# Attention ahead of S5 and GLA, with S5's weight-only matrices made in paced steps and kept in DRAM

## The chip, the cores and the metric

The kernel runs on one core of one Trainium2 chip. The metric is the device time of one execution in microseconds (us), as the median of several runs. The engines are TensorE (PE: matmuls, and PEld its weight loads), VectorE (DVE), ScalarE (ACT), GpSimd (POOL), and SyncE (SP), which issues nearly all DMAs.

## The reference

Two layers run over 640 tokens, 512 of a sample and 128 of a prompt, of width 1024. Each layer normalises, projects once into all inputs, runs three branches, gates and merges them:

```python
h = rms_norm(x, p['norm_w']) * (1.0 + scale) + shift
(gq, gk, gv, gaf, gab, g_gate, mq, mkv, mkr, m_gate, su, s_gate, merge) = split_cols(h @ p['w_in'], IN_SPLITS)
o_a, st_gla = gla_mixer(gq, gk, gv, gaf, gab, ..., ctx_gla)      # chunked linear attention, 4 heads
o_b, st_mla = mla_mixer(mq, mkv, mkr, ..., rope, ctx_mla)        # softmax attention, 4 heads
o_c, st_s5 = s5_mixer(su, ..., ctx_s5)                           # complex diagonal scan, then a GLU
g_a, g_b, g_c = jnp.split(jax.nn.sigmoid(merge), 3, axis=-1)
mixed = (g_a * ((o_a * jax.nn.silu(g_gate)) @ p['w_bo_gla'])
         + g_b * ((o_b * jax.nn.silu(m_gate)) @ p['w_bo_mla'])
         + g_c * ((o_c * jax.nn.silu(s_gate)) @ p['w_bo_s5']))
y = x + gate * (mixed @ p['w_out'])
```

S5 turns its weights (a, dt, B, C) into powers of the discretised a and products of those with B and C. These depend on no token. The three branches depend on `h` alone, so their order is free.

## The kernel before

Activations lie with the channels on the partitions, as 8 tiles of 128 x 640. Every f32 product is made of three matmuls of split values: `split` writes `hi` with ACT and `lo = x - hi` with DVE. Weights come as 128 x 512 halves (`wraw`, one DMA from `wpk`), and `half` splits each into `whi` and `wlo`. A projection `projh_` is 8 k-steps of 6 matmuls of 128 x 320 and yields after each k-step.

The order of TensorE is the order in which the program is written. The other engines and the DMA queue are ordered by a scheduler of the framework, which uses priorities and its own timeline. Where a branch is a chain of small dependent steps, the program calls `fill(n)`, which takes n k-steps from the generators in `self.stand`, so that TensorE has projections to do meanwhile. The tables `FILL`, `FM` (attention) and `FG` (GLA head) hold the n of each place.

The order in a layer is: `h`; the S5 input projection `s5_su`; the S5 kernel (`s5_kernel`: per group of channels C-outers `s5qk`, made by three DVE operations each, times `s5rd`); `s5_in`, `s5_z` (B-outers `s5r`, transposed), powers (`s5_pow`), scan (`s5_scan`), output (`s5_y`, from the matrices `s5m`, which pass through DRAM as `kd`, and `s5qy`, which pass as `qd`) and GLU; attention (`mla_qkv`, `mla_heads`); GLA (`gla_in`, four times `gla_head`); then `merge(0)` and `out_proj`. Filler is what the later branches need: latents and gates (`mla_raw`), eight merge gates (`mer_early(0)`), `merge(2)` along attention, `merge(1)` along GLA. While layer 0 runs `out_proj`, `s5_open(1)` makes the S5 coefficients of layer 1 and steps its `s5_kernel` three tiles in.

A GLA head goes: cumulated gates, exponentials `eb`, `kd`, `kr`, `fill(FG[0])`, scores `att`, `fill(FG[1])`, transposes of `kr`, `fill(FG[2])`, state products and the chain of 16 updates of `st` on DVE (each needs the one before in its direction), `fill(FG[3])`, output matmuls, norm `gon`, `fill(FG[4])`, transposes of `gon` into `og`.

Of the kernel before, what the change touches and what calls it, by code (L numbers as in the profile page):

```python
# [10 lines left out]
F32 = mybir.dt.float32  # L11
# [8 lines left out]
L = 2  # L20
# [4 lines left out]
NB = 16  # L25
# [159 lines left out]
FILL = (17, 2, 1, 4, 2, 10, 10, 1, 7, 3)  # L185
FM = (1, 6, 1, 4, 2, 4, 3, 2, 1)
FG = (7, 2, 2, 5, 5)
# [14 lines left out]
class Prog:  # L202
# [113 lines left out]
    def consts(self):  # L316
# [20 lines left out]
        self.qd = [self.dr.tile([8, 2, 128, 512], F32, name=f"qd{l}") for l in range(L)]  # L337
        self.sud = [self.dr.tile([NT, 512], F32, name=f"sud{l}") for l in range(L)]
        self.gd = [self.dr.tile([8, 128, NT], F32, name=f"gd{l}") for l in range(L)]
        self.md = [self.dr.tile([8, 128, NT], F32, name=f"md{l}") for l in range(L)]  # L340
# [136 lines left out]
    def gate_(self, name, og=False):  # L477
# [3 lines left out]
        if og:  # L481
            g = self.ogp.tile([128, NT], F32, name="og", tag="og", bufs=12)
        else:
            g = self.th.tile([128, NT], F32, name="gt", tag="gt", bufs=2)
        self.V.scalar_tensor_tensor(self.v2(g), self.v2(th), 1.0, ps, op0=ALU.add, op1=ALU.mult)
        return g
# [11 lines left out]
    def mer_early(self, b):  # L498

        for j in range(8):  # L500
            self.mid = True
            th = yield from self.mer(b, j)
            self.S.dma_start(self.md[self.l][j], th)
            self.early.add((b, j))
            self.mid = False
# [10 lines left out]
    def finish_tile(self, g):  # L516
        while self.mid:
            yield next(g)

    def merge(self, b, og, mode):  # L520
        V = self.V
        if mode:
            parts = []
            for t in og:
                hi, lo = self.og(), self.og()
# [4 lines left out]
        if mode == 0:  # L530
            self.mix = self.mx()[:, :5120].rearrange("p (k t) -> p k t", k=8)
        for j in range(8):
            if (b, j) in self.early:
                th = self.th.tile([128, NT], F32, name="th", tag="th", bufs=2)
                self.S.dma_start(th, self.md[self.l][j])
            else:
                th = yield from self.mer(b, j)
                yield True
            ps = yield from self.proj_([self.half(f"bo{b}_{j // 2}", j % 2)], og)
            m = self.mix[:, j, :]  # L540
            if mode == 0:
# [43 lines left out]
    def cmul(self, V, p, o_r, o_i, ar, ai, br, bi, shape):  # L585
        pat = "p (a b) -> p a b"
        t1 = p.tile([128, shape[1] * shape[2]], F32, name="cm1", tag="cm1")
        t2 = p.tile([128, shape[1] * shape[2]], F32, name="cm2", tag="cm2")
        t1, t2 = (t.rearrange(pat, a=shape[1]) for t in (t1, t2))
# [3 lines left out]
        t3 = p.tile([128, shape[1] * shape[2]], F32, name="cm1", tag="cm1")  # L593
        t4 = p.tile([128, shape[1] * shape[2]], F32, name="cm2", tag="cm2")
        t3, t4 = (t.rearrange(pat, a=shape[1]) for t in (t3, t4))
# [20 lines left out]
    def exp_(self, V, p, out, x):  # L616

        t = p.tile([128, 3, 64], F32, name="ex", tag="ex")
        k, r, y = t[:, 0], t[:, 1], t[:, 2]
# [8 lines left out]
        e = p.tile([128, 64], I32, name="exi", tag="exi")  # L628
# [3 lines left out]
    def s5_prep(self, l, vec, p, pz, ptmp):  # L632

        V = self.V
        n0 = VEC["B1"][0]
        bs, cs = pz.tile([128, 1024], F32, name="s5b"), p.tile([128, 1024], F32, name="s5c")
        with self.tc.high_priority(5200):
            for i, t in enumerate((bs, cs)):
                self.S.dma_start(t, self.a["vec"][l][:, n0 + 1024 * i:n0 + 1024 * i + 1024])
        self.B1, self.B2, self.C1, self.C2 = (t[:, 512 * i:512 * i + 512].rearrange("p (g c) -> p g c", c=16)  # L640
                                              for t in (bs, cs) for i in range(2))
# [992 lines left out]
```

## Time and profile before

| | before |
|---|---|
| median of 3 runs | 1600.47 us (1599.04 to 1603.54) |
| profiled execution | 1601.22 us, span 1599.4 us |
| mean granted TensorE clock | 0.981 |
| PE, DVE, ACT, POOL busy | 95%, 66%, 40%, 3% of the span |
| matmuls | 11334 |

The time of the profiled execution holds 1.8 us around the span. A busy PE is not a PE at its peak: matmuls are pipelined, so two that overlap count once, and at half clock the same matmuls are busy for longer. The granted clock is a mean over a stretch of the two levels 2.4 GHz (1.00) and 1.2 GHz (0.50).

### The profile page before, as it was taken

How to read it: one execution, taken by the hardware profiler on the slowest of the kernel's cores; microseconds unless marked ns; L12 is line 12 of the kernel's file. 1: busy time of each engine (PE TensorE's matmuls, PEld its weight loads, DVE VectorE, ACT ScalarE, POOL GpSimd, SP SyncE). 2: the span in 40 equal slices, each digit the busy share in tenths (PEclk: the TensorE clock that was granted, in tenths of full speed). 3: DMA queues.
4: the chain of work that ended last, by engine and by line, in shares of the span. 5: the costliest groups of instructions: out<-in, count | busy, mean ns of one | idle time of the engine just before them, and what ended most of it. 6: DMA issues, size and time to landing. Idle time of an engine off the chain costs nothing. (4 is left out here: it accounts for less than half of the span.)

```text
span 1599.4 us, 28779 instructions
## 1 busy us (share of the span) xinstructions
PE 1516.4 (95%) x11334; PEld 1438.9 (90%) x11334; DVE 1056.4 (66%) x2435; ACT 631.8 (40%) x1171; POOL 47.7 (3%) x48
## 2 busy tenths in 40 slices
PE   4999999999998898999799999999999989989999
PEld 3789999999997888898697999999999979889998
DVE  8986992367566436879987579724766663477762
ACT  3335223555444353333223542244544442634331
POOL 0000000012000000000000000000210000000000
PEclk9999999999999899999899999999999999999999
DMA  9451435323311121227553432442332122212253
GB/s 339 169 152 42 154 114 157 117 86 115 113 55 58 46 75 54 65 85 255 206 193 92 124 112 90 138 151 76 106 120 93 55 66 66 68 60 60 93 166 107
DMA packets 108792, 179.73 MB, mean 112 GB/s; under 512 B 12656, under 2 KB 30768, under 8 KB 108656
## 3 DMA queue, kind: packets, MB, share of 16 engines
q1 hardware_dynamic: 108656, 177.89, 34.3%
q8 instruction: 89, 1.46, 0.4%
q14 instruction: 47, 0.39, 0.1%
HBM read 149.23 MB, written 28.61 MB: 111 GB/s over the span
## 5 line engine op out<-in xcount | busy, mean ns | idle before, releaser
L245 PE MATMUL pj<-h,whi 128*128 128x320 f32 x3456 | 664.1, 313 | 0.0
L245 PEld LDWEIGHTS pj<-h,whi 128*128 128x128 f32 x3456 | 541.2, 189 | 6.6 <-issue 5.1
L227 ACT ACTIVATE whi<-wraw 128x512 fp32r<-128x512 f32 x326 | 205.0, 631 | 508.4 <-PE pj L245 359.2
L245 PE MATMUL pj<-h,wlo 128*128 128x320 f32 x1728 | 397.3, 310 | 0.0
L236 DVE TENSOR_TENSOR wlo<-wraw,whi 128x512 fp32r<-128x512 f32 x326 | 223.9, 688 | 245.5 <-ACT whi L227 238.6
L245 PEld LDWEIGHTS pj<-h,wlo 128*128 128x128 f32 x1728 | 290.3, 188 | 0.0
L245 PE MATMUL pj<-og,whi 128*128 128x320 f32 x736 | 142.1, 313 | 0.3 <-DVE og L236 0.3
L245 PEld LDWEIGHTS pj<-og,whi 128*128 128x128 f32 x736 | 114.7, 188 | 4.7 <-ACT whi L227 1.6
L245 PE MATMUL pj<-whi,h 128*128 128x512 f32 x256 | 87.1, 401 | 6.3 <-ACT h L230 5.7
L245 PE MATMUL pj<-og,wlo 128*128 128x320 f32 x384 | 87.5, 309 | 0.0
L245 PEld LDWEIGHTS pj<-whi,h 128*128 128x128 f32 x256 | 48.7, 192 | 19.5 <-ACT h L230 6.3
L245 PEld LDWEIGHTS pj<-og,wlo 128*128 128x128 f32 x384 | 64.2, 188 | 0.0
L230 ACT ACTIVATE P<-bank,smx 128x384 f32<-128x384 f32 x64 | 36.4, 575 | 56.0 <-DVE smx L1215 56.0
L236 DVE TENSOR_TENSOR Ptl<-bank,Pth 128x512 fp32r<-128x512 f32 x48 | 32.1, 689 | 34.3 <-ACT Pth L227 33.7
L230 ACT ACTIVATE th<-pj 128x640 f32<-128x640 f32 x72 | 49.6, 689 | 5.5 <-PE pj L245 5.4
L245 PE MATMUL pj<-wlo,h 128*128 128x512 f32 x128 | 50.8, 397 | 0.0
L245 PE MATMUL pj<-s5g,whi 128*128 128x320 f32 x256 | 48.1, 310 | 0.0
L245 PE MATMUL bank<-s5qy,mx 128*80 128x128 f32 x256 | 46.1, 302 | 0.0
L227 ACT ACTIVATE Pth<-bank 128x512 fp32r<-128x512 f32 x48 | 27.5, 596 | 41.3 <-PE bank L1236 41.1
L1236 PE MATMUL bank<-c,P 128*128 128x128 f32 x192 | 32.2, 304 | 11.9 <-ACT P L230 5.3
L1211 DVE TENSOR_REDUCE smx<-bank 128x1 f32<-128x384 f32 (+1 forms) x72 | 36.2, 524 | 9.0 <-PE bank L245 8.1
L1400 DVE SCALAR_TENSOR_TENSOR st<-st,bl,bank 64x128 f32<-64x128 f32 x112 | 38.9, 347 | 3.6
(349 smaller groups left out, 2324.2 us busy)
## 6 DMA issues: line engine op xcount, KB each, us to landing
wraw<-wpk SPq DMA_DIRECT2D x358, 256.0 KB, 2.7
og<-wpk SPq DMA_DIRECT2D x48, 256.0 KB, 5.1
qd<-s5qk SPq DMA_DIRECT2D x32, 256.0 KB, 2.2
s5qy<-qd SPq DMA_DIRECT2D x32, 256.0 KB, 4.1
gd<-gt SPq DMA_DIRECT2D x16, 320.0 KB, 2.5
gt<-gd SPq DMA_DIRECT2D x16, 320.0 KB, 3.1
md<-th SPq DMA_DIRECT2D x16, 320.0 KB, 2.3
th<-md SPq DMA_DIRECT2D x16, 320.0 KB, 3.1
```

Of the source, the lines that this page charges most:

```text
L227: self.A.activation(out, in_, AF.Copy, scale=scale)
L230: self.A.activation(out, in_, f, **kw)
L236: (eng or self.V).tensor_tensor(lo, src, hi.bitcast(F32), op=ALU.subtract)
L245: self.T.matmul(out, lhsT, rhs, start=start, stop=stop, skip_group_check=True, **kw)
L1211: V.tensor_reduce(mx[:, i:i + 1], ps[:, 0:w], axis=AX.X, op=ALU.max)
L1236: self.T.transpose(pt[:, nq * i + 128 * qi:nq * i + 128 * qi + 128], pr[qi][:, 128 * k:128 * k + 128], self.ident)
L1400: V.scalar_tensor_tensor(out, st[r, c, :], bl[r, c:c + 1], pu[c][r], op0=ALU.mult, op1=ALU.add)
```

## The change

The branches run in the order attention, S5, GLA. The latents are projected right behind `s5_su`, and everything else that `h` feeds (12 gates, 24 merge gates, the last third of the modulation) becomes filler from there on, stored to DRAM (`gd`, `md`) and loaded again by `gate_in` and `merge`. `merge(1)` and `merge(2)` are the filler of the GLA heads. `s5_ahead` makes all S5 matrices that depend on weights alone in about 134 steps per layer, paced by `bg`: 60 at the start of layer 0, then one per k-step of `s5_su`, 0.75 per step of the latents, 0.5 per filler step. It stores them to DRAM (`qd`, `rd`, `r0d`, `ptd`), and `s5_kernel`, `s5_z` and `s5_scan` load them. The groups of `s5_kernel` stand between the steps of the scan, and nothing of layer 1's S5 is made at the end of layer 0.

```diff
-FILL = (17, 2, 1, 4, 2, 10, 10, 1, 7, 3)
+FILL = (8, 2, 1, 3, 2, 10, 10, 1, 7, 3)
+COEF = 60
+PACE = (1, 0.75, 0.5)
 FM = (1, 6, 1, 4, 2, 4, 3, 2, 1)
-FG = (7, 2, 2, 5, 5)
+FG = (5, 2, 2, 4, 4)
...
+    def s5_ahead(self, l, vec, x):
...
+        def outers(m, coef, dst):
+            for n in range(16):
...
+                for _ in self.outer(V, v4(o[n % 2]), v4(o[2]), c[0], c[1], m[0][:, 4 * b:4 * b + 4], m[1][:, 4 * b:4 * b + 4], sh):
+                    yield
+                self.S.dma_start(dst[b, d], o[n % 2])
...
         for b in range(8):
-            q = [self.s5_q(V, p, b, d, f"s5qk{d}", 4) for d in range(2)]
+            q = []
             for d in range(2):
-                self.S.dma_start(self.qd[l][b, d], q[d].rearrange("p a b c -> p (a b c)"))
+                q.append(p.tile([128, 4, 8, 16], F32, name=f"s5qk{d}", tag=f"s5qk{d}", bufs=2))
+                self.S.dma_start(q[d], self.qd[l][b, d].rearrange("p (a b c) -> p a b c", a=4, b=8))
+            yield
...
+    def gates_(self):
+
+        for i in (0, 1, 2, 3, 8, 9, 10, 11, 4, 5, 6, 7):
+            g = yield from self.gate_(("mg%d", "gg%d", "sg%d")[i // 4] % (i % 4))
+            self.S.dma_start(self.gd[self.l][i], g)
+            self.gdone.add(i)
             yield True
...
     def fill(self, n):
 
         for _ in range(n):
+            self.bg(PACE[2])
...
+    def bg(self, n):
+
+        self.owed += n
+        while self.owed >= 1:
+            self.owed -= 1
+            next(self.ahead, None)
...
+        for _ in self.mla_raw():
+            self.bg(PACE[1])
+        self.stand = [self.gates_(), self.alternate(self.mer_early(1), self.ada(l, self.vec, 2)), self.mer_early(2), self.mer_early(0)]
+        fill(FILL[6])
...
                 ogb = self.mla_heads(p)
-        self.stand = [g for g in self.stand if g is not early] + [self.finish_tile(early)]
-        fill(1000)
-        self.stand = [self.merge(1, ogb, 1)]
-        fill(1)
+        run(self.ahead)
+        with ExitStack() as eg:
+            with pool("s5a") as pa:
+                with pool("s5k") as pk:
+                    kern = self.s5_kernel(pk)
+                    with pool("s5i") as p, tc.high_priority(2000):
+                        self.s5_in(pa, p, fill)
+                        self.s5_z(p, fill)
+                    with pool("s5s") as p:
+                        self.s5_pow(p)
+                        for n, _ in enumerate(self.s5_scan(p)):
+                            fill(FILL[3])
+                            if n % 2:
+                                next(kern, None)
+                        run(kern)
...
         with pool("gla") as pa:
             with pool("glb") as p:
                 self.gla_in(pa, p)
+            fill(1000)
+            part = lambda: self.hp.tile([128, NT], F32R, name="h", tag="h", bufs=16)
+            self.stand = [self.merge(1, ogb, part, True), self.merge(2, ogc)]
             with pool("glc") as p:
                 oga = [self.gla_head(p, h) for h in range(4)]
         fill(1000)
-        out = self.merge(0, oga, 2)
+        out = self.merge(0, oga, self.og)
...
-        self.s5_open(l + 1)
-        kern = self.s5[-1]
         run(self.alternate(out, self.ada(l + 1, self.nvec, 0)))
-        for j, _ in enumerate(self.out_proj()):
-            if j >= 3:
-                next(kern, None)
+        run(self.out_proj())
```

The first place is the end of the last attention head of layer 0 on TensorE: the last products with the probabilities (`Pth`, `Ptl`), the transpose of the prompt's (`Pp`) and its product with the values. Before:

```order
L245 MATMUL bank<-Ptl,vh 128x256 x2
L245 MATMUL bank<-Pth,vh 128x256
L245 MATMUL bank<-Pth,vl 128x256
L245 MATMUL bank<-Pth,vh 128x256
L245 MATMUL bank<-Pth,vl 128x256
L245 MATMUL bank<-Ptl,vh 128x256 x2
L1236 MATMUL bank<-c,Pp 128x128
L245 MATMUL bank<-Pt,vt 128x128
```

And now:

```order
L247 MATMUL bank<-Ptl,vh 128x256 x2
L247 MATMUL pj<-h,whi 128x320 x4
L247 MATMUL pj<-h,wlo 128x320 x2
L247 MATMUL bank<-Pth,vh 128x256
L247 MATMUL bank<-Pth,vl 128x256
L247 MATMUL bank<-Pth,vh 128x256
L247 MATMUL bank<-Pth,vl 128x256
L247 MATMUL bank<-Ptl,vh 128x256 x2
L1266 MATMUL bank<-c,Pp 128x128
L247 MATMUL pj<-h,whi 128x320 x4
L247 MATMUL pj<-h,wlo 128x320 x2
```

Projections (`pj<-h`) stand between the steps now, also in the last head, where there were none.

The second place is the last GLA head of layer 0 on TensorE, from the output matmuls (`st,gqd`) to the transposes of the normed output (`c,gon`). Before:

```order
L245 MATMUL bank<-st,gqd 64x128 x10
L245 MATMUL pj<-h,whi 128x320 x4
L245 MATMUL pj<-h,wlo 128x320 x2
L245 MATMUL pj<-og,whi 128x320 x4
L245 MATMUL pj<-og,wlo 128x320 x2
L245 MATMUL pj<-og,whi 128x320 x4
L245 MATMUL pj<-og,wlo 128x320 x2
L245 MATMUL pj<-og,whi 128x320 x4
L245 MATMUL pj<-og,wlo 128x320 x2
L245 MATMUL pj<-og,whi 128x320 x4
L245 MATMUL pj<-og,wlo 128x320 x2
L1440 MATMUL bank<-c,gon 128x128 x5
```

And now, with the first rows of `merge(0)` behind (`og` there is the split GLA output):

```order
L247 MATMUL bank<-st,gqd 64x128 x10
L247 MATMUL pj<-og,whi 128x320 x2
L247 MATMUL pj<-tmp,whi 128x320 x2
L247 MATMUL pj<-og,wlo 128x320 x2
L1470 MATMUL bank<-c,gon 128x128 x5
L247 MATMUL pj<-og,whi 128x320 x4
L247 MATMUL pj<-og,wlo 128x320 x2
```

One filler step stands there instead of five, and `merge(0)` follows the transposes at once. In the other heads it is four instead of five.

The third place is the DMA queue of SP in layer 0 ahead of the S5 output: the stores of the kernel sums (`kd`), the loads of `s5m` made from them, and those of `s5qy`. Before:

```order
L772 DMA kd_98<-s5ks 128x1x240
L796 DMA s5cr<-sud_102 80x8x128 x3
L266 DMA wraw<-wpk 128x512 x4
L796 DMA s5cr<-sud_102 80x8x128
L266 DMA wraw<-wpk 128x512 x5
L777 DMA s5m<-kd_98 16x8x128
L266 DMA wraw<-wpk 128x512
L777 DMA s5m<-kd_98 16x8x128 x8
```

And now:

```order
L828 DMA kd_98<-s5ks 128x1x240 x4
L268 DMA wraw<-wpk 128x512
L833 DMA s5m<-kd_98 16x8x128 x7
L268 DMA wraw<-wpk 128x512
L833 DMA s5m<-kd_98 16x8x128 x5
L268 DMA wraw<-wpk 128x512
L833 DMA s5m<-kd_98 16x8x128 x4
L268 DMA wraw<-wpk 128x512
L978 DMA s5qy_5624<-qd_100 128x512
L978 DMA s5qy_5626<-qd_100 128x512
```

The stores stood ahead of the whole of `s5_in` and `s5_z`; now they stand behind the scan's last kernel group, and the loads right behind them.

## Rows read from the trace of the kernel before

**Rows 1.** The page: busy us, share of the span, instructions of each engine.
```profile
PE 1516.4 (95%) x11334; PEld 1438.9 (90%) x11334; DVE 1056.4 (66%) x2435; ACT 631.8 (40%) x1171; POOL 47.7 (3%) x48
```

**Rows 2.** Timeline of PE under dense filler: start, us, engine, line, operation.
```profile
235.85 0.75 PE L245 MATMUL pj<-h,whi 128*128 128x320 f32 x4
...
236.73 0.75 PE L245 MATMUL pj<-h,whi 128*128 128x320 f32 x4
```

**Rows 3.** Waits of PE, whole span: total us, times, longest.
```profile
PE bank L245 <- DVE s5qk L718: 15.2, 4, 12.2
...
PE bank L245 <- DVE st L1400: 12.3, 8, 2.9
```

**Rows 4.** Windows in attention: length, busy PE PEld DVE ACT POOL, clock, DMA share, GB/s.
```profile
440.00:480.00 40.00, 40.00 (x287) 39.62 (x286) 25.01 (x61) 17.56 (x41) 0.00 (x0) 1.00 0.17 55
...
507.00:541.00 34.00, 23.11 (x121) 19.83 (x121) 20.20 (x51) 13.28 (x34) 0.38 (x2) 0.80 0.08 24
...
1300.00:1330.00 30.00, 20.90 (x108) 18.51 (x108) 17.21 (x46) 12.93 (x32) 1.10 (x3) 0.77 0.16 47
```

**Rows 5.** Timeline of PE: first h of layer 0, and end of attention.
```profile
31.75 0.79 PE L245 MATMUL pj<-whi,h 128*128 128x512 f32 x1 [5.70 <-ACT h L230]
...
517.64 0.30 PE L1236 MATMUL bank<-c,P 128*128 128x128 f32 x1 [3.12 <-ACT P L230]
```

**Rows 6.** Windows at the layer boundary, columns as in rows 4.
```profile
780.00:800.20 20.20, 8.00 (x56) 7.74 (x55) 20.05 (x39) 3.37 (x5) 0.00 (x0) 0.79 0.46 154
800.20:806.00 5.80, 5.80 (x46) 5.42 (x47) 5.43 (x11) 0.37 (x1) 0.00 (x0) 0.57 0.47 181
806.00:846.00 40.00, 38.96 (x420) 35.76 (x419) 27.63 (x56) 9.29 (x17) 1.16 (x1) 0.96 0.60 203
```

**Rows 7.** Windows of the four GLA heads, layers 0 and 1, columns as in rows 4.
```profile
597.40:713.00 115.60, 107.49 (x981) 101.27 (x981) 85.56 (x195) 43.29 (x84) 4.66 (x4) 0.97 0.21 68
1385.70:1499.80 114.10, 106.00 (x981) 99.79 (x980) 85.33 (x193) 43.24 (x84) 4.66 (x4) 0.99 0.19 60
```

**Rows 8.** Waits of PE in layer 0's GLA heads: total us, times, longest.
```profile
PE bank L245 <- DVE st L1400: 6.2, 4, 2.9
...
PE bank L1382 <- DVE kr L1358: 0.7, 2, 0.4
PE bank L1440 <- DVE gon L1434: 0.3, 1, 0.3
```

**Rows 9.** DVE at the boundary by group: busy us, mean ns, idle before it.
```profile
L716 DVE TENSOR_TENSOR s5qk<-s5pw,s5c 128x512 f32<-128x512 f32 x10 | 6.4, 686 | 0.4 <-PE bank L245 0.4
```

**Rows 10.** DVE in layer 0's GLA heads by group, columns as in rows 9.
```profile
L236 DVE TENSOR_TENSOR wlo<-wraw,whi 128x512 fp32r<-128x512 f32 x21 | 14.4, 687 | 6.8 <-ACT whi L227 6.6
...
L546 DVE TENSOR_TENSOR mx<-mx,tmp 128x640 f32<-128x640 f32 x6 | 4.9, 816 | 0.0
```

**Rows 11.** Timeline of PE: output matmuls of the first and the last GLA head.
```profile
621.36 2.40 PE L245 MATMUL bank<-st,gqd 128*64 128x128 f32 x20 [2.95 <-DVE st L1400]
...
707.16 1.31 PE L245 MATMUL bank<-st,gqd 128*64 128x128 f32 x20 [1.12 <-DVE st L1400]
```

**Rows 12.** Timeline of PE behind the last GLA head of layer 0.
```profile
713.46 0.82 PE L245 MATMUL pj<-h,whi 128*128 128x320 f32 x4
...
727.45 0.57 PE L245 MATMUL pj<-og,whi 128*128 128x320 f32 x2 [0.26 <-DVE og L236]
```

**Rows 13.** Timeline of SP's queue ahead of the S5 output of layer 0.
```profile
99.39 1.96 SPq L772 DMA_DIRECT2D kd<-s5ks  x3
...
160.08 4.51 SPq L777 DMA_DIRECT2D s5m<-kd  x8
...
169.03 2.33 SPq L947 DMA_DIRECT2D s5qy<-qd  x5
```

**Rows 14.** DMA issues: count, KB each, median us to landing.
```profile
s5qy<-qd SPq DMA_DIRECT2D x32, 256.0 KB, 4.1
...
kd<-s5ks SPq DMA_DIRECT2D x8, 120.0 KB, 3.6
```

More of the change, by code (lines that the diff above doesn't have):

```diff
@@ L514, in alternate, with merge @@
         yield from b
[L516 to L520, printed above, removed]
+    def merge(self, b, og, split=None, first=False):
         V = self.V
-        if mode:
+        if split:
             parts = []
             for t in og:
-                hi, lo = self.og(), self.og()
+                hi, lo = split(), split()
                 self.split(hi, lo, t)
@@ new lines, in powers @@
+    def powers(self, at, ab, tmp):
+        V = self.V
+        for i in range(2):
+            V.tensor_copy(at(i, 0, 1)[:, 0], ab[:, i])
+        n = 1
+        while n < NB:
+            sh = [128, n, 64]
+            a, b = (at(i, 0, n) for i in range(2))
+            c, d = (at(i, n - 1, n).to_broadcast(sh) for i in range(2))
+            t1, t2 = (t[:, 0:n] for t in tmp)
+            o = [at(i, n, 2 * n) for i in range(2)]
+            V.tensor_tensor(t1, a, c, op=ALU.mult)
+            V.tensor_tensor(t2, b, d, op=ALU.mult)
+            V.tensor_tensor(o[0], t1, t2, op=ALU.subtract)
+            yield
+            V.tensor_tensor(t1, a, d, op=ALU.mult)
+            V.tensor_tensor(t2, b, c, op=ALU.mult)
+            V.tensor_tensor(o[1], t1, t2, op=ALU.add)
+            yield
+            n *= 2
@@ L714, in outer @@
+    def outer(self, eng, out, tmp, s1, s2, m1, m2, shape):
         b = lambda s: s[:, :, :, None].to_broadcast(shape)
@@ L993, in s5_glu @@
         for i in range(4):
-            if i == 1:
-                for n in norms:
-                    next(n, None)
-            g = gates[i]
+            g = self.gate_in(8 + i)
             us = self.units(f"glu{i}")
@@ L1570, in layer @@
-        self.stand = [g for g in self.stand if g is not early] + [
-            self.finish_tile(early), self.alternate(self.merge(2, ogc, 0), self.ada(l, self.vec, 2)), early]
+            self.make_h(x, rs, range(0, 8 if l else 4))
+        if l:
+            self.ahead = self.s5_ahead(l, self.vec, self.mx())
+        with pool("su") as p:
+            with tc.high_priority(2000):
+                su = self.s5_su(p)
+            for k in range(8):
+                with tc.high_priority(2000):
+                    next(su, None)
+                if l == 0 and k < 3:
+                    both(rest, (3, 3, 20)[k])
+                    if k == 2:
+                        with tc.high_priority(5000):
+                            self.make_h(x, rs, range(4, 8))
+                self.bg(PACE[0])
+            with tc.high_priority(2000):
+                run(su)
```

329 lines of the change are left out of this document (140 added, 189 removed).

## The prediction

> **What bounds the kernel now.** I read the page first: TensorE (PE) is busy 95% of the span [rows 1], so the kernel is a stream of matmuls and the question is where that stream stands still or runs at half clock. Six matmuls of 128x320, one filler step, start every 0.88 us when nothing interferes (235.85 to 236.73) [rows 2]. The change neither adds nor removes a matmul, so only the standstill can change. Then the waits of PE: the largest that the change can touch are 15.2 us on s5qk and 12.3 us on st [rows 3]. Last, PE's busy time stage by stage, which shows what the list of waits hides, the half clock behind a wait.
>
> Three places matter. (a) The end of attention. From 440 to 480 PE is busy 40.00 of 40 us, since a projection stands between any two steps of a head. From 507 to 541 the projections are used up: 23.11 of 34 at a mean clock of 0.80, and in layer 1 20.90 of 30 at 0.77 [rows 4]; the single longest wait there is 3.12 us for the exponentials [rows 5]. A mean of 0.80 is 40% of the time, 13.6 us, at 1.2 instead of 2.4 GHz, which costs about half, 6.8. So layer 0 loses 10.9 + 6.8 = 17.7 and layer 1 9.1 + 6.9 = 16.0: 33.7 together. (b) The layer boundary. VectorE (DVE) makes the C-outers of layer 1 there and is busy 20.05 of 20.20 us, while PE has 8.00; the 5.8 us behind it run at 0.57 [rows 6]. (c) The GLA heads: 115.6 and 114.1 us for four heads, DVE busy 85.6 of them [rows 7]. Here every stretch of filler is already a little too short: PE waits for st at each head, for kr at two, for gon at one [rows 8].
>
> **The change, part by part.**
>
> *Attention with filler to its end.* All gates and merge gates are now behind attention as filler, and the last head keeps a projection between its steps, as the first piece of order shows. By [rows 4] that is the state of 440 to 480, a loss of zero. DVE gets work in addition: an outer is three operations of 0.69 us [rows 9], and in layer 0 74 of 134 paced steps remain after the first 60, 51 us spread over projections and attention, where DVE had 25.0 of 40 us. It fits, but a softmax operation can now stand behind one. I leave 2 us of loss per layer: gain 30 (bounds 20 and 33.7).
>
> *The boundary.* The 12.2 us on s5qk [rows 3] go, and with them the half clock behind: (1 − 0.57) x 5.8 = 2.5 [rows 6]. The kernel groups were also what PE had to do while the first h tiles of layer 1 were made; without them a wait for h appears. The nearest row is the same wait in layer 0, 5.70 us [rows 5]; here only part of that chain is uncovered, so I take 3 (bounds 1 and 7). Net gain 11.7. The other three waits on s5qk, 15.2 − 12.2 = 3.0, stood at the start of layer 0 and go too. Sum of the gains: 30 + 11.7 + 3 = 44.7.
>
> *GLA heads with less filler.* The table gives 17 steps per head instead of 21, and only 65 are there (33 of one merge, 32 of the other), against 84: 19 steps, 16.7 us of matmuls, leave each layer's stage and cover attention instead. If the stage were bound by PE, it would shrink to 98.9. It is not: the steps removed are those ahead of kr (FG[0], two), of st (FG[3], one) and of gon (FG[4], one), exactly the waits of [rows 8]. What it can shrink to is set by DVE. The filler of before brought 21 weight splits, 6 adds and as many tmp of the same size [rows 10]; two merges bring 16 splits, 8 products and 8 tmp with 8 adds: −5 x 0.687 + 12 x 0.816 = +6.4 us, so 92.0 us of DVE work where there were 85.6. DVE was at 74% of the stage because it too waits in the chain of a head; with less filler to alternate with I take 85%, that is 108 us. The stage then shrinks by 7.6 instead of 16.7 and loses 9.1: 18 for both layers (bounds 0 and 33). Where a wait of a head passes some 2 us the clock falls: behind the 2.95 us wait the 20 state matmuls take 2.40 us, and 1.31 behind a wait of 1.12 [rows 11]. I add 3 for such drops (bounds 0 and 14).
>
> The Trainium skill, "TensorE: Matmul & The Clock Gate", section on HAM oscillation, says that a kernel whose bursts of matmuls are each followed by a wait pays the fall of the clock at every one. The rows bear that out for the first head; the three later ones share 6.2 − 2.95 = 3.3 us of waits [rows 8] and the head of [rows 11] behind 1.12 us keeps its clock. By the page every head of the changed kernel would pay; that is part of the second rival.
>
> *merge(0) right behind the last head.* Before, PE had filler from 713.46 to 727.45 while the last og was finished and split, and then still waited 0.26 us [rows 12]. Now no filler is left, and the tiles for the split come free only when merge(2) ends. Two DVE operations of 1.0 us together for og and one split on each of ScalarE and DVE (0.8 each) must pass before the last quarter of the first projection: 3 us per layer, 6 in all (bounds 2 and 20).
>
> *S5 kernel inside the scan.* Its eight groups now stand between scan steps, and the loads of s5m and s5qy move from far ahead (issued at 160 in layer 0, while the scan ran) to right behind them (third piece of order). After the last s5ks four stores must issue (3 in 1.96, so 2.6) and land (3.6), then 8.95 us pass from the first s5m issue to the first s5qy (160.08 to 169.03), which lands after 4.1 [rows 13, 14]: 19.3, and about 1 for the copy ahead. PE has 20 filler steps between the last group and the first y matmul: 17.6. So at least 2.7 us are open, more if DVE, which has the whole scan in front of the last s5ks, is late. I take 5 with the clock behind it, 10 for both layers (bounds 0 and 20). That the loads of r for s5_in queue behind others on SP I put at 2 in all (bounds 0 and 8).
>
> The Trainium skill, "DMA: Bandwidth & Descriptors", section on rules for kernel authors, asks to issue a DMA early, compute, and wait late. This part does the reverse. By the page alone the two landing times would lie open, 7.7 us per layer, 15.4 instead of 10; the rows of the queue decide, since PE's filler covers most of them.
>
> *Costed at nothing:* the 180 more DMA issues (the queues move only 55 GB/s late in attention [rows 4]), the powers and r by DMA, gates reloaded from DRAM. Their cover is the filler; if it were gone, one landing of 3 us each would show.
>
> **Sum.** Gains 44.7. Losses 18 + 3 + 6 + 10 + 2 = 39. Net −5.7. From 806 to 846 the clock is 0.96 and PE has 38.96 of 40 [rows 6], 1.0 + 1.6 us lost among the remaining kernel groups, of which 2 should go too: −7.7. The profiled execution took 1601.2 us (span 1599.4 and 1.8 around it), 0.7 over the median of the runs: 1600.5 − 7.7 = 1592.8, **1593 us**.
>
> **Rivals.**
> 1. *GLA stays bound by PE.* DVE's 92 us lie under 98.9, and if the scheduler fills its gaps, the stage shrinks by the whole 16.7. Against it: DVE would have to be busy 93%, which it reaches only in stages without a chain. The 18 + 3 go: 1572. Chance 0.18.
> 2. *Slower: the chain of a head does not shorten at all.* The waits of [rows 8] are already waits, and where PE waits already, taking filler away only lengthens the wait. Stage stays at 115.6: 2 x 7.6 = 15 more, and with waits of 2 us and over at kr, st and gon the clock falls in each head; [rows 11] price a fall at 2.40 − 1.31 = 1.1 and as much again in the filler behind, 8 times at most, of which I count half, 8. 1593 + 23 = 1616. It turns the sign as soon as the stage is above 112 us. For it: the order of DVE still has fillers between the updates of st. Against: with fewer filler operations per chain it should move a little. Chance 0.30.
> 3. *The gain doesn't come:* the paced steps push the softmax back so that PE waits inside every head as it did in the last. At a third of the 134 steps in the way of a softmax (0.69 each) that is 30 us per layer at worst, 10 likely: 1593 + 20 = 1613. Against it, DVE at 25 of 40 us. Chance 0.08.
> 4. My forecast, 1583 to 1604: chance 0.44.
>
> **How the numbers follow.** Runs of one kernel differ by 0.3% (1599.0 to 1603.5), so a change under 4.8 us is none. The forecast lies on the line's faster side: of its 0.44 about 0.29 is under 1595.7, 0.13 within, 0.02 above. Rival 1 adds 0.18 to faster, rivals 2 and 3 mostly to slower (0.02 each within). Faster 0.47, the same 0.17, slower 0.36. The range 1572 to 1617 takes in rival 1 and nearly all of 2; beyond it lie the ends where y, GLA and h all go one way.
>
> **What would show it.** Right: PE full to the end of both attention stages with no half clock; no wait on s5qk at the boundary, but one of about 3 us on h; GLA stages of about 108 us with DVE near 85%; a wait of 3 to 5 us on s5qy at the first y and of about 3 at the first og of merge(0). Wrong: GLA under 100 or over 113; waits on P or smx in the early heads; a wait on s5m or s5qy over 10 us; new waits in the first 100 us, which I left as they are.

## The result, and the profile after

The change makes the kernel slower: 1700.88 us (1693.34 to 1701.62, 4 runs) against 1602.01 (1599.04 to 1605.46) beside it, ratio 1.0606, interval 1.0568 to 1.0644. The forecast was 1593, a small gain, and its range ended at 1617. No matmul was added, so these 99 us are standstill and half clock: in the two profiled executions PE stood idle for 83.0 us of the span before and for 150.4 us now, and the same 11334 matmuls kept it busy for 1516.4 and for 1548.9 us. The page's row of busy time, which answers to [rows 1]:

```profile
PE 1548.9 (91%) x11334; PEld 1468.1 (86%) x11334; DVE 1058.3 (62%) x2435; ACT 635.6 (37%) x1171; POOL 56.0 (3%) x48
```

The same instructions on every engine; DVE is no busier than before, only at other places. The waits of PE over the whole span (answers to [rows 3]; total us, times, longest):

```profile
PE bank L247 <- DVE st L1430: 23.1, 8, 3.2
PE bank L1412 <- DVE kr L1388: 18.5, 8, 4.3
...
PE bank L1470 <- DVE gon L1464: 12.8, 6, 4.6
PE bank L1213 <- DVE qt L1098: 11.9, 6, 3.7
PE bank L860 <- ACT s5cg L229: 10.4, 2, 5.7
PE bank L247 <- DMA s5qy<-qd: 10.0, 2, 5.0
PE bank L394 <- ACT tmp L229: 8.8, 4, 4.6
...
PE bank L1266 <- DVE P L1252: 5.1, 2, 2.8
```

The 15.2 us on `s5qk` are gone. In their place stand four families: `st`, `kr`, `gon` in the GLA heads (54.4 us, where there were 14.3), `qt` and `P` in attention (17.0), `s5cg` and `tmp` at the start of S5 (19.2), `s5qy` at its output (10.0). The windows of the changed kernel (columns as in [rows 4]): the end of attention of layer 0 and of layer 1, the first heads of layer 1, the start of S5's output, the boundary, the four GLA heads of each layer:

```profile
320.00:358.00 38.00, 36.87 (x273) 34.05 (x272) 18.77 (x47) 15.52 (x35) 0.00 (x0) 1.00 0.43 139
...
1150.00:1196.00 46.00, 45.61 (x337) 42.18 (x335) 22.93 (x56) 19.27 (x42) 0.00 (x0) 1.00 0.41 137
...
1008.00:1040.00 32.00, 18.98 (x104) 17.23 (x105) 29.77 (x72) 8.01 (x18) 2.88 (x2) 0.79 0.34 121
...
492.00:506.00 14.00, 8.96 (x53) 8.38 (x52) 0.69 (x1) 1.23 (x2) 0.00 (x0) 0.76 0.85 262
...
800.00:880.00 80.00, 74.96 (x578) 70.30 (x577) 39.84 (x85) 25.28 (x44) 1.17 (x1) 0.96 0.52 172
...
638.10:762.70 124.60, 95.33 (x863) 87.95 (x863) 91.25 (x201) 38.49 (x76) 5.10 (x4) 0.92 0.29 90
1480.80:1604.80 124.00, 95.12 (x860) 87.52 (x859) 91.06 (x201) 38.51 (x76) 5.11 (x4) 0.92 0.28 89
```

The forecast gains came. The end of attention is full at full clock (1.1 and 0.4 us open), and around the boundary PE stands still for 5.0 of 80 us, 2.04 of them for h, where [rows 6] had 13.2 of 66 (20.20 − 8.00 + 40 − 38.96). But layer 1's first heads have PE at 18.98 of 32 us with the clock at 0.79, and each GLA stage has become longer than in [rows 7], not shorter, with 118 matmuls fewer in it.

What DVE does at layer 1's first heads, by group (busy us, mean ns, idle before it):

```profile
L791 DVE TENSOR_TENSOR mx<-mx 128x512 f32<-128x512 f32 x9 | 6.2, 685 | 0.0
L789 DVE TENSOR_TENSOR mx<-mx 128x512 f32<-128x512 f32 x9 | 6.2, 684 | 0.0
L787 DVE TENSOR_TENSOR mx<-mx 128x512 f32<-128x512 f32 x8 | 5.5, 684 | 1.0 <-DMA rd<-mx 1.0
```

These are the paced outer products: 17.9 of DVE's 29.77 us there. In layer 0 the paced powers stand there instead, as the timeline of DVE shows ahead of the first head's longest wait (start, us):

```profile
184.30 0.42 DVE L773 TENSOR_TENSOR mx<-mx 128x256 f32<-128x256 f32 x1
184.64 0.42 DVE L774 TENSOR_TENSOR mx<-mx 128x256 f32<-128x256 f32 x1
184.97 1.00 DVE L1195 SCALAR_TENSOR_TENSOR qt<-qt,hrs,rows 128x96 f32<-128x96 f32 x4
...
186.43 0.42 DVE L775 TENSOR_TENSOR mx<-mx 128x256 f32<-128x256 f32 x1
...
187.24 0.28 DVE L1098 TENSOR_TENSOR qt<-rp,rp 128x128 f32<-128x128 f32 x1
187.45 0.41 DVE L777 TENSOR_TENSOR mx<-mx 128x256 f32<-128x256 f32 x1
```

PE took that `qt` at 187.58 after 3.67 us. The last GLA head of layer 0 on DVE, from `kr`'s first part to its end, for which PE waited 4.31 us until 740.89:

```profile
732.90 0.81 DVE L537 SCALAR_TENSOR_TENSOR tmp<-th,pj 128x640 f32<-128x640 f32 x1
733.63 0.68 DVE L238 TENSOR_TENSOR wlo<-wraw,whi 128x512 fp32r<-128x512 f32 x1
734.34 0.98 DVE L1383 TENSOR_TENSOR kr<-bl,bank 64x512 f32<-64x512 f32 x2
...
735.53 0.83 DVE L538 TENSOR_TENSOR mx<-mx,tmp 128x640 f32<-128x640 f32 x1
...
736.94 0.29 DVE L1383 TENSOR_TENSOR kr<-bl,bank 64x128 f32<-64x128 f32 x1
...
737.67 0.81 DVE L537 SCALAR_TENSOR_TENSOR tmp<-th,pj 128x640 f32<-128x640 f32 x1
738.40 0.68 DVE L238 TENSOR_TENSOR wlo<-wraw,whi 128x512 fp32r<-128x512 f32 x1
...
740.01 0.83 DVE L1388 TENSOR_TENSOR kr<-kr,gkd 128x640 f32<-128x640 f32 x1
```

Five operations of the merges, 3.8 us, stand between the steps of `kr`.

### The profile page after: what moved, and what is told of

It reads as the page before. It is cut to its first block, busy times and chain, and to the rows that moved or that the text cites. A ratio compares the mean times of both kernels' runs of the same rounds, so it can differ in the third digit from the quotient of the medians.

```text
span 1699.3 us, 29201 instructions
## 1 busy us (share of the span) xinstructions
PE 1548.9 (91%) x11334; PEld 1468.1 (86%) x11334; DVE 1058.3 (62%) x2435; ACT 635.6 (37%) x1171; POOL 56.0 (3%) x48
## 4 chain that ended last, share of the span: by engine, by line
PE 72%; DVE 16%; DMA 6%; issue 2%; ACT 1%; SPq 1%; POOL 0%; POOLq 0%; DVEq 0%; ACTq 0%
PE pj L247 52%; PE bank L247 16%; DVE st L1430 2%; DVE wlo L238 2%; DMA wraw<-wpk 2%; PE bank L1266 1%; PE bank L876 1%; DVE mx L791 1%; DMA s5cr<-sud 1%; DVE kr L1383 1%; DMA s5c<-r0d 1%; DVE mx L789 1%; DVE mx L787 1%; DVE tmp L537 1%; SPq L833 1%
## 5 line engine op out<-in xcount | busy, mean ns | idle before, releaser
L247 PE MATMUL pj<-h,whi 128*128 128x320 f32 x3712 | 722.5, 316 | 1.2 <-ACT whi L229 1.2
L247 PEld LDWEIGHTS pj<-h,whi 128*128 128x128 f32 x3712 | 587.3, 191 | 10.7 <-issue 7.7
L247 PE MATMUL pj<-h,wlo 128*128 128x320 f32 x1856 | 430.2, 312 | 1.4 <-DVE wlo L238 1.4
L247 PEld LDWEIGHTS pj<-h,wlo 128*128 128x128 f32 x1856 | 315.2, 190 | 1.8 <-DVE wlo L238 1.8
L247 PE MATMUL pj<-og,whi 128*128 128x320 f32 x480 | 101.7, 333 | 2.2 <-DVE og L238 2.2
L247 PEld LDWEIGHTS pj<-og,whi 128*128 128x128 f32 x480 | 80.9, 203 | 8.1 <-DVE og L238 3.0
L247 PE MATMUL pj<-og,wlo 128*128 128x320 f32 x256 | 61.2, 322 | 0.0
L247 PEld LDWEIGHTS bank<-s5qy,mx 128*80 128x80 f32 x256 | 42.4, 231 | 11.0 <-issue 11.0
L787 DVE TENSOR_TENSOR mx<-mx 128x512 f32<-128x512 f32 x64 | 43.8, 685 | 5.8 <-DMA qd<-mx 3.0
L247 PEld LDWEIGHTS pj<-og,wlo 128*128 128x128 f32 x256 | 45.8, 200 | 0.0
L791 DVE TENSOR_TENSOR mx<-mx 128x512 f32<-128x512 f32 x64 | 43.9, 685 | 0.5
```

Source lines behind the costliest of these rows:

```text
L247: self.T.matmul(out, lhsT, rhs, start=start, stop=stop, skip_group_check=True, **kw)
L787: eng.tensor_tensor(out, b(s1), d(m1), op=ALU.mult)
L791: eng.tensor_tensor(out, out, tmp, op=ALU.add)
```

## The experiments

The theory that these lines suggest: four separate losses, each a piece of work or a load that now stands in front of a step PE has no filler left for. The rival: the losses are one thing, matmuls that moved to the end of attention and are missing everywhere else, so that mending one place opens another. A kernel that was run once is compared with the changed kernel's 1700.88. That kernel's own four runs lie up to 8.3 us apart (1693.34 to 1701.62), and the kernel before gave 1598.6 to 1606.3 beside the others, so differences under some 8 us are not told apart in such a run.

**Attention: the paced steps.** `a1_ahead_third` leaves out two of the three operations of every paced outer product:

```diff
         eng.tensor_tensor(out, b(s1), d(m1), op=ALU.mult)
         yield
-        eng.tensor_tensor(tmp, b(s2), d(m2), op=ALU.mult)
         yield
-        eng.tensor_tensor(out, out, tmp, op=ALU.add)
         yield
```

> The changed kernel with the outers of the paced steps cut to the first of their three DVE operations (the S5 output is no longer the reference's); steps, stores and pacing stay. Theory A: the attention stages lose time because the paced steps take DVE where the chains of attention need it. Then the waits on qt at the first head (8 us in layer 1, 4 in layer 0) and on P in layer 1's first head (8 us) fall to 2 us or less each, and the time falls by 20 to 30, to 1670 to 1680. Rival B: DVE's load has nothing to do with it; the waits come from the new order of projections and of DVE's queue. Then both stay and the time is within 8 of 1700.

1680.43 us, 20.5 less. PE's waits for `qt` fall from 11.9 to 3.4 us, those for `P` on DVE are gone from the list, and layer 1's first heads are nearly full (1008 to 1040 us again; the first `qt` matmul of the layer starts 2 us earlier than in the changed kernel):

```profile
1008.00:1040.00 32.00, 30.58 (x200) 29.84 (x201) 23.82 (x60) 13.10 (x31) 0.00 (x0) 0.95 0.31 105
```

So DVE's load by paced steps makes this loss. `c3_no_pace_qkv` stops the pacing during the projections of attention, and `d1_attn_first` ranks attention's instructions ahead of the paced steps wherever both are ready:

```diff
+                self.pace = 0
                 self.mla_qkv(pa, p)
+                self.pace = PACE[2]
```

```diff
-                self.mla_qkv(pa, p)
+                with tc.high_priority(2000):
+                    self.mla_qkv(pa, p)
...
-            with pool("mlc") as p:
+            with pool("mlc") as p, tc.high_priority(2000):
```

> The changed kernel with no paced step during mla_qkv; what is left is made later, in the heads and ahead of S5. Theory A: the wait for qt at the first head (8 us in layer 1, 4 in layer 0) is DVE busy with paced steps in just that stretch; then it falls to under 2 and 3 us, and the time by 8 to 14 if the heads bear the steps. Rival B: the steps shift their cost: the heads of layer 1 wait on P for as much more, and the time is within 5 of 1700.

> The changed kernel with the instructions of attention's projections and heads preferred by the scheduler over the paced steps wherever both are ready. Theory (the paced VectorE steps stand in the queue ahead of operations of the heads' chain): the preference moves them behind, the waits for qt (11.9 us in the changed kernel) and for P (5.1 us) shrink to below half, and the time falls by up to the 20 us that thinner steps gave, to 1680 to 1692. Rival (a step goes in because the chain's operation is not yet ready when VectorE is free, so a preference among ready operations decides little): qt and P waits stay within 3 us, the time is 1697 to 1705.

1701.77 and 1696.66; the longest wait for `qt` stays at 3.7 us. The pace sets only where a step is written. Its inputs are ready early and the scheduler runs it in the first gap of DVE, which a head's chain leaves while it waits for ACT or GpSimd; the chain's next step then finds DVE taken. Both times came out as the rivals had them, near the changed kernel's. In `c3` not even the steps moved: from 1000 to 1070 us L787 runs 14 times in both kernels, and from 1070 to 1200 never.

**The output of S5.** `a2_kern_each` makes one kernel group ahead of every scan step instead of every second:

```diff
-                            if n % 2:
-                                next(kern, None)
+                            next(kern, None)
```

> The changed kernel with one kernel group per scan step instead of one in two, so that the last is done some 25 us of filler earlier. Theory A: the first y matmul waits for s5qy (5.0 us per layer) because the stores of the kernel sums and the loads behind them start too late. Then that wait falls under 1 us and the clock stays up: 12 to 15 us less, 1686 to 1689. Rival B: DVE with the scan is late, or the queue of SP is full with other transfers; then the wait stays at 4 us or over.

1680.55, 20.3 less; the wait for `s5qy` (10.0) is gone. In the changed kernel the loads follow the stores behind the last group, and PE is out of filler before they land; the 14 us from 492 on run at a mean clock of 0.76:

```profile
499.39 1.32 PE L247 MATMUL bank<-s5qy,mx 128*80 128x128 f32 x4 [5.04 <-DMA s5qy<-qd]
```

**The start of S5.** `c1_s5in` gives `s5cr`, the token rows of S5's input, four buffers instead of two (and `s5r` four instead of six, for space), and spreads the late modulation between the gates:

```diff
-            cr = p.tile([NC8, 8, 128], F32, name="s5cr", tag="s5cr", bufs=2)
+            cr = p.tile([NC8, 8, 128], F32, name="s5cr", tag="s5cr", bufs=4)
...
-        self.stand = [self.gates_(), self.alternate(self.mer_early(1), self.ada(l, self.vec, 2)), self.mer_early(2), self.mer_early(0)]
+        self.stand = [self.alternate(self.gates_(), self.ada(l, self.vec, 2)), self.mer_early(1), self.mer_early(2), self.mer_early(0)]
```

> The changed kernel with all four s5cr loads in buffers of their own (s5cr 4 buffers, s5r 4 instead of 6) and with the last third of the modulation (ada 2) spread over the gates instead of the merge gates, so that it ends in mid-attention. Theory A: what is lost around the start of S5 (10 us per layer: PE on s5cg 4.7 and 5.7, on the copy tmp of ada 2 behind an s5cg on ScalarE 3.4 and 4.6, with the clock behind each) comes from the late s5cr loads. Then the waits on s5cg and tmp fall from 19 to under 5 us, and the time by 15 to 22, to 1679 to 1686. Rival B: the loads land late because the DMA queues are full at that time; then the waits on s5cg stay over 8 us.

1671.22, 29.7 less; of the waits for `s5cg` and `tmp` 0.5 and 0.9 us are left. What was mended is seen on ACT in the changed kernel, where `s5cg` stood 4.33 us for its rows and PE 4.70 us behind it (until 377.86):

```profile
376.75 1.06 ACT L229 ACTIVATE s5cg<-s5cr 80x1024 f32<-80x1024 f32 x1 [4.33 <-DMA s5cr<-sud]
```

The load of that last `s5cr` was issued only at 369.81 us, after the second `s5cg`, whose buffer it takes, had ended (368.11), and landed 6.9 us later. Which of the two edits gave how much was not separated.

**The GLA heads.** `a3_mer0_in_gla` puts the eight projections of `mer_early(0)` into the heads as filler and runs `merge(2)` ahead of them and `merge(1)` behind; `a4_fg0` has no filler in the heads:

```diff
...
-            self.stand = [self.merge(1, ogb, part, True), self.merge(2, ogc)]
+            self.stand = [self.merge(2, ogc, None, True)]
+            fill(1000)
+            self.stand = [self.mer_early(0)]
...
+        run(self.merge(1, ogb, part))
```

```diff
-FG = (5, 2, 2, 4, 4)
+FG = (0, 0, 0, 0, 0)
```

> The changed kernel with the GLA heads filled by eight merge gates (64 steps of plain projections) instead of merge(1) and merge(2) (65 steps); merge(2) runs ahead of the heads, merge(1) behind them; FG is not changed. Theory A: the heads take 124 us because each merge tile brings two or three more DVE operations into the chain of a head. Then, with the same number of steps, the four heads take 108 to 114 us and DVE's share falls. Rival B: it is the number of filler steps at each wait (FG) alone; then the heads stay at 121 to 126. The whole time says less, since attention and S5 have 57 us less to do between their steps: 1700 to 1730.

> The changed kernel with no filler inside the GLA heads (FG all 0); the two merges run behind the heads. It measures the bare chain of a head. Theory A: filler operations of DVE lengthen the chain, so the bare head takes 21 to 24 us, four 85 to 95, against 124. Rival B: the chain of a head is 28 to 31 us by itself, and filler only covers it: four heads 112 or more. The merges add some 60 us behind, so the whole kernel takes 1730 to 1770.

The windows of the four heads, first of the one, then of the other:

```profile
639.80:745.40 105.60, 88.69 (x863) 81.58 (x863) 77.06 (x182) 45.16 (x86) 4.66 (x4) 0.98 0.28 88
```

```profile
646.70:752.60 105.90, 52.05 (x479) 44.00 (x479) 63.82 (x161) 27.60 (x59) 4.66 (x4) 0.55 0.06 17
```

With as many matmuls as in the changed kernel the heads took 19.0 us less when the filler was projections rather than merges. So matmuls do not set the stage. The kernel as a whole got slower, 1710.8: S5 lost this filler and waited 27.5 us for `s5m`. The bare heads (1773.8 in all) took 105.9, but at a clock of 0.55, so that number is no floor; it lay between the two values expected. DVE is busy for 60% of it: 13.2 us less DVE work than with projections as filler bought no shorter stage. Whether the half clock or something else in the chain holds it there, no run separates.

Two light edits, `c4_add_on_pool` (the merges' adds on GpSimd) and `g1_fill_last` (the heads' filler ranked behind the heads' own steps wherever both are ready):

```diff
-                V.tensor_tensor(m, m, t, op=ALU.add)
+                self.G.tensor_tensor(m, m, t, op=ALU.add)
```

```diff
-                    next(self.stand[0])
+                    if self.low:
+                        with self.tc.high_priority(-self.low):
+                            next(self.stand[0])
...
```

> The changed kernel with the add of merge(2) and merge(0) on GpSimd instead of DVE (0.82 us each on DVE, about 8 of them in the third and fourth GLA head). Theory A: each DVE operation of filler that stands in the chain of a head lengthens it by its own time; then the third and the fourth head shorten by 2 to 4 us each and the first two stay, 6 to 14 us less over both layers. Rival B: the chain is not bound by DVE's queue; then heads three and four keep 29 to 35 us.

> The changed kernel with the filler of the four GLA heads (the merges, their weight splits and adds) ranked behind the heads' own operations wherever both are ready. Theory (the stage is the chain of a head, with operations of the merges standing in it on VectorE): fewer of them stand in the chain, the four heads take 112 to 119 us for 124.6, and the time falls by 8 to 20 us. Rival (they go in while the chain's operation is not ready, so ranking changes little): 122 to 126 us for the four heads, the time within 4 us of the changed kernel's 1700.9.

1700.75 and 1697.15: no change to be told, and the waits for `st`, `kr` and `gon` with the ranking are 23.7, 18.4 and 11.8. In `c4` DVE's work in the first layer's heads hardly fell, to 89.12 us of 122.4, although 6.5 us of adds had left it: the splits rose from 685 to 764 ns each and the additions into `att` from 484 to 638 (see the last section). So `c4` says little of what DVE's work costs. `f1_thin_evac` goes at the length of the operations instead. It keeps every operation but takes the merges' results from PSUM in 64 of 640 columns (the rest of the mix is zero):

```diff
...
+                c = slice(0, 32 if b else 320)
-                V.scalar_tensor_tensor(self.v2(t), self.v2(th), 1.0, ps, op0=ALU.add, op1=ALU.mult)
-                V.tensor_tensor(m, m, t, op=ALU.add)
+                V.scalar_tensor_tensor(self.v2(t)[:, :, c], self.v2(th)[:, :, c], 1.0, ps[:, :, c], op0=ALU.add, op1=ALU.mult)
+                V.tensor_tensor(self.v2(m)[:, :, c], self.v2(m)[:, :, c], self.v2(t)[:, :, c], op=ALU.add)
```

> The changed kernel with the 24 VectorE operations that take the merges' results from PSUM and add them, which stand in the four GLA heads, cut to 64 of 640 columns (the other columns of the mix are zero, so the output is not the reference's); matmuls, weight splits and order of emission stay. Theory (the heads are one chain of waits with these 19.5 us of VectorE work standing in it, on top of the 106 us that the bare heads took): 105 to 111 us for the four heads instead of 124.6, and a time of 1661 to 1677. Rival (the chain is long because of the matmuls and weight splits of the merges, whatever their results cost): 119 us or more, and a time above 1688.

1669.23, 31.7 less, and the heads of both layers:

```profile
639.30:747.30 108.00, 91.29 (x863) 83.69 (x863) 76.92 (x201) 38.49 (x76) 4.66 (x4) 0.95 0.35 103
1464.90:1574.60 109.70, 93.24 (x863) 85.64 (x863) 76.92 (x201) 38.47 (x76) 4.67 (x4) 0.95 0.33 100
```

Matmuls, splits and order stayed, 14.3 us of DVE work went (91.25 to 76.92), and each stage fell by 16.6 and 14.3 us. It is DVE's work in the chain, and nearly one for one over this range; `a4` shows that this does not go on below.

**Together.** `e1_three_mended` joins `a2`, `c1` and `d1`; `e2_and_fill_last` adds `g1`; `f2_all_mended` is `e1` with the outer products of `a1` and the thin results of `f1`.

> The changed kernel with three edits together: one kernel group ahead for each scan step, four buffers for the S5 weight rows with the late adaptive projection spread between the gate projections, and attention ranked ahead of the paced steps. Theory (the losses of the stages are separate): the gains add, 20 us of the first and 30 us of the second, and what the third gives alone (0 to 20), so 1631 to 1652. Rival (the filler that covers one stage is taken from another, so gains are given back as with the kernel groups moved in the kernel before): 1655 to 1672. Both leave the GLA heads at about 120 us each layer, so that it does not reach the 1602 us of before.

> The same three edits and the filler of the GLA heads ranked behind the heads' operations. Theory (merge operations stand in the GLA chain): 8 to 20 us below the run with the three edits alone. Rival (the ranking changes little): within 4 us of it.

> Everything that was found, in one kernel: the three edits of the earlier combination, the paced outer products cut to one of their three VectorE operations, and the merges' results cut to 64 columns (output not the reference's). Theory (the causes found are all that the change lost): from the 1658 us of the three edits, 30 to 38 us less for the heads' VectorE work and 10 to 20 us less for the paced products, so 1600 to 1618, about the kernel before. Rival (something not yet found costs 20 us or more, or the gains are given back elsewhere): 1625 or more.

`e1`: 1658.34 (1656.48 to 1662.78), ratio 1.0332, interval 1.0311 to 1.0352: 42.5 us won of the 50.0 that its two effective parts gave alone. So most adds; whether the rest is given back, as the rival had it (1655 to 1672), single runs do not tell. `e2`: 1655.47, 1.0284 to 1.0343, no difference to be told. `f2`: 1604.54 beside 1604.72 of the kernel before on that chip. The four causes alone gave 20.5, 20.3, 29.7 and 31.7, 102.2 together; in one kernel 96.3. That is as much as the change lost, but not proof that nothing else costs time. The two thin parts leave out work that the kernel before did as well, and they were not tried on it, so the sum tells how much lies there, not that each of these us belongs to the change. And `f2` has the gains at the end of attention and at the boundary in it, so about as much loss must still stand beside them. Part of it is seen in the heads, which PE still does not fill:

```profile
609.80:717.10 107.30, 91.04 (x863) 83.47 (x863) 76.88 (x201) 38.41 (x75) 4.66 (x4) 0.96 0.35 103
1400.60:1510.10 109.50, 93.23 (x863) 85.47 (x863) 76.88 (x201) 38.48 (x76) 4.66 (x4) 0.95 0.33 101
```

PE stands still for 32.5 us in these two stages, against 16.2 in [rows 7].

**Work moved rather than left out.** `h1_merge_side_on_pool` is `e1` with the adds and the weight splits of the two filler merges on GpSimd; `h2_paced_mult_on_pool` puts the second operation of each paced product there too:

```diff
-                V.tensor_tensor(m, m, t, op=ALU.add)
+                (self.G if b else V).tensor_tensor(m, m, t, op=ALU.add)
...
-            ps = yield from self.proj_([self.half(f"bo{b}_{j // 2}", j % 2)], og)
+            ps = yield from self.proj_([self.half(f"bo{b}_{j // 2}", j % 2, eng=self.G if b else None)], og)
```

```diff
-        eng.tensor_tensor(tmp, b(s2), d(m2), op=ALU.mult)
+        self.G.tensor_tensor(tmp, b(s2), d(m2), op=ALU.mult)
```

> The three-edit combination (1658 us) with the adds and the weight splits of the two merges that fill the GLA heads moved from VectorE to GpSimd: 8 adds of 0.82 us and some 16 splits of 0.685 us less on VectorE in each stage, 17.5 of its 91 us. Theory (VectorE work in the heads' chain costs its own length): the thin-evacuation run bought 17 us a stage with about 17 us of VectorE work, so up to 17 us a stage, 34 in all: 1624 to 1640. Rival (an operation costs only where it stands in the chain, and the splits, whose result is wanted late, and the adds stand mostly beside it; GpSimd's 1.9 us an add and a later split hold up the merges' matmuls): less than 8 us in all, 1650 or more.

> The run before and one of the three operations of each paced outer product on GpSimd as well. Theory (a paced step costs the heads of attention what it takes of VectorE): a third of the paced products' VectorE time off, some 22 us a layer, 3 to 10 us less than the run with the merges' side work on GpSimd alone. Rival (the heads' own reciprocal roots are on GpSimd too, 24 of 1.5 us, and now wait behind products of 1.9 us or more each): the waits for qt and P grow, the time is 3 us or more above it.

`h1`: 1644.58 (1640.68 to 1646.03), ratio 1.0241, interval 1.0204 to 1.0278: 13.8 less than `e1`, between theory and rival. It is the best whole kernel of the changed order, and still slower than before. Its heads:

```profile
618.40:733.00 114.60, 91.40 (x863) 84.31 (x863) 82.60 (x180) 38.41 (x75) 34.76 (x25) 0.96 0.33 100
1430.70:1545.60 114.90, 91.40 (x863) 84.32 (x863) 82.59 (x180) 38.42 (x75) 34.74 (x25) 0.96 0.32 97
```

In `e1` they take 124.8 and 126.3 us with 91.11 us of DVE work each. So DVE lost 8.5 us a stage instead of the 17.5 expected, because what stayed on it took longer (last section), and the stages became 10.2 and 11.4 us shorter. `h2`: 1658.99, ratio 1.0331 (1.0296 to 1.0366): 14.4 more than `h1`. The time is as its rival had it, the waits are not: those for `qt` fell from 13.3 to 10.7 us and those for `P` from 4.5 to 3.4. PE stood idle as long as in `h1` (118.2 and 117.6 us); what grew is its busy time for the same matmuls, from 1521.2 to 1536.2 us, at a mean clock of 0.965 for 0.978. Which step brought the clock down is not shown; what DVE lost is in the last section.

**The kernel before, one part alone.** `b1_no_kern_in_out` takes the kernel groups of layer 1 out of `out_proj` in the kernel before:

```diff
-        for j, _ in enumerate(self.out_proj()):
-            if j >= 3:
-                next(kern, None)
+        run(self.out_proj())
...
-            step(self.s5[-1], 4)
+            step(self.s5[-1], 1)
```

> The kernel before with one thing of the change alone: no kernel group inside out_proj, and one step instead of four ahead of h in layer 1; the groups run behind s5_su as in layer 0. The boundary alone: the wait of 12.2 us for s5qk and the half clock behind it go, a wait for h of 2 to 4 us appears: 8 to 13 us less than the kernel before. Rival: the wait moves with the groups, to behind s5_su, because DVE has the same outers to make; then no change within 4 us.

1602.6 beside 1598.57: nothing won, although the wait on `s5qk` fell from 15.2 to 3.3 us. The groups now use up filler that covered attention later; the waits of PE for P, 7.6, 5.3 and 3.4 us before, became 8.2, 6.3 and 5.5. That is 3.7 us of the 11.9, and PE's busy time for the same matmuls rose by 7.3 us (1516.4 to 1523.7). So the boundary's gain is at least in part a loan, and here the rival of one stock of filler is right in part.

## Why the prediction was wrong

Two of the signs of being wrong that the prediction named came: GLA stages over 113 us and waits on P in the early heads.

*End of attention, +30, and the sentence "It fits".* The tail gained what was forecast. The step that failed is the cover for the paced steps: DVE's 25.0 of 40 us was read as 15 us of room. That room is the gaps of a chain, and a step that fills one delays the chain's next step. Nor were the steps "spread over projections and attention". The 51 us were those of layer 0; layer 1 has no 60 steps made in advance, and of its 32 products 12 ran from 900 to 960 us, 5 up to 1000, 15 up to 1070 and none behind (counted at L789), so that DVE was busy for 29.77 of 32 us at the first heads. Rival 3 named this at 0.08 and a price of 20; thinner steps gave back 20.5.

*Boundary, +11.7.* Right: 13.2 us of standstill in 66 became 5.0 in 80, 8.2 less, and of half clock some 8.3 us by the clocks of [rows 6] became 3.2 (0.96 over 80 us), 13 together; the new wait for h is 2.0 us for 3 forecast. The 3 us at the start of layer 0 did not come: the waits for `s5qk` went, but those for h there rose from 6.3 to 9.1 us.

*GLA heads, loss 18 + 3.* This is the largest miss, 108 us expected for each stage and 124.6 and 124.0 measured, 33 us in all. DVE's work was sized well (92.0 forecast, 91.25 measured). The step that failed is "with less filler to alternate with I take 85%". DVE's share did not move: 85.56 of 115.60 before [rows 7], 91.25 of 124.60 after, 77.06 of 105.60 with projections as filler, 76.92 of 108.00 with thin results: 74, 73, 73 and 71%, and 72% in `h1`. Had I kept the 74% that stood in the rows, 92.0 / 0.74 = 124 us would have come out. Rival 2, that the stage does not shrink at all, pointed the right way and stopped short, because it let the chain stand still where merges brought more DVE work into it. Waits of 4.3 us at `kr` and a clock of 0.92 followed.

The Trainium skill, "TensorE: Matmul & The Clock Gate", section on HAM oscillation, had been weighed as speaking for rival 2. The stage's clock of 0.92 for 0.97 and 0.99 before agrees with it.

*merge(0), 6.* The wait for the first `og` in layer 0 was 1.09 us for 3 forecast. But the 38 us from 762 on, behind a wait of 4.6 us for `gon`, ran at 0.89, some 4 us of half clock, so the term was a little short and not the trouble.

*S5 output, 10.* The mechanism and the wait were right (5.04 us for 5 "with the clock behind it"), the size was not: `a2` gave 20.3. The stretch behind the wait ran at a mean of 0.76, which I had counted inside the 5.

*Start of S5, 2.* The step that failed is "That the loads of r for s5_in queue behind others on SP I put at 2 in all". The rows of r were not late; those of `s5cr` were, which had only two buffers, and ACT stood behind them with everything else. In the kernel before, S5 ran elsewhere; PE waited 1.8 us for `s5cg` in all there, and none of the rows read holds that wait. `c1` gave 29.7.

*The sum.* Of the gains some 43 came (30 and 13), so with 98.9 us more in the end the losses were near 142, for 39 forecast; the single edits account for 102 of them, and the rest was not taken apart. I costed each moved part against the filler it was next to, and gave the same filler away more than once: [rows 8] showed waits for `st`, `kr` and `gon` already open, and the 19 steps taken from there could not come free.

## What to carry to other kernels

In a stage that is a chain across engines, an engine's idle share is not room: keep the share that the trace shows, divide the changed work by it, and expect the stage to move with it. The share was 70 to 75% in the heads of seven kernels with filler (the one before, the changed one, `a3`, `e1`, `f1`, `f2`, `h1`) but 60% in `a4`, without filler, so it carries over between like stages only. A pace in the program's text and a rank among ready steps moved nothing; work to be hidden there would have to be held back by what it depends on, which no run tried. Count filler as one stock: what covers a new place is taken from an old one, and before believing a gain, look up which wait there was nearly open already.

## What the runs showed of the hardware

GpSimd operations held DVE up. In `h1` the last GLA head of layer 0 has, on DVE and on GpSimd:

```profile
706.48 2.22 DVE L1405 TENSOR_TENSOR att<-am,am 64x320 f32<-64x320 f32 x2
```

```profile
706.65 1.71 POOL L538 TENSOR_TENSOR mx<-mx,tmp 128x640 f32<-128x640 f32 x1 [1.96 <-DVE tmp L537]
```

The pair of additions into `att` takes 0.98 us in the changed kernel; here the second ended only after GpSimd's add did. By group, over the first layer's heads in `h1`:

```profile
L1383 DVE TENSOR_TENSOR kr<-bl,bank 64x512 f32<-64x512 f32 (+1 forms) x16 | 7.7, 483 | 0.3
...
L1405 DVE TENSOR_TENSOR att<-am,am 64x320 f32<-64x320 f32 x8 | 6.1, 763 | 0.1
L1387 DVE TENSOR_TENSOR kd<-kd,gkd 128x640 f32<-128x640 f32 x4 | 4.1, 1020 | 0.0
```

In `e1` these take 484, 482 and 808 ns. The operation with an input in PSUM kept its time, the two with both inputs in SBUF lost 281 and 212 ns each. A short operation with one input, L1461 on `gss`, rose as well, from 170 to 506 ns. In `h2` the paced products on DVE rose likewise, by group over the span:

```profile
L787 DVE TENSOR_TENSOR mx<-mx 128x512 f32<-128x512 f32 x64 | 59.4, 928 | 6.5 <-DMA qd<-mx 2.7 <-DMA rd<-mx 2.5 <-DMA r0d<-mx 1.0
```

from 685 ns in `e1`, while GpSimd needed 1404 ns for what DVE does in 683. So a third of DVE's paced work moved away took 44 us off it and put 15.6 back at this line alone.

The Trainium skill, "SBUF — State Buffer", section "Who interferes with whom", says that a DVE instruction with two SBUF inputs contends with a GpSimd instruction that reads SBUF, and that the port pair they share is an exclusive lock. The rows with two inputs agree: the second addition into `att` ended at 708.70 us, GpSimd's add at 708.36.
